# One product of each pair of gate and up units split into seven of half the size, from the fifth unit on

## The chip, the cores and the metric

The kernel runs on one core of a Trainium2 chip. TensorE (PE) multiplies, VectorE (DVE) and ScalarE (ACT) do the element-wise work on PSUM and SBUF, GpSimd (POOL) takes some sums in SBUF, and SyncE (SP) issues most transfers. The metric is the device time of one execution in microseconds.

## The reference

A trunk of two layers over x (1024 tokens, 1024 channels). Each layer has a token mixer (attention) and a SwiGLU channel mixer; the change is in the first half of the channel mixer alone:

```python
x = x + jnp.concatenate([y_tok, y_mem], axis=-1) @ w_out[i]
h = rmsnorm(x, norm_ffn[i])
gu = h @ w_gate_up[i]
x = x + (jax.nn.silu(gu[..., :D_FF]) * gu[..., D_FF:]) @ w_down[i]
```

D_FF is 2816, so gate and up are each 22 units of 128 columns. All is float32; a product is made of three fp32r products of high and low halves (hi and lo: `hi` on ACT rounds, `lo` on DVE takes the rest).

## The kernel before

A layer runs in stages, one after the other, and PE is kept busy across them: the input projection and attention, the output projection, gate and up, and down. Tokens lie along the free axis in two halves of 512 (HS).

Gate and up treat each unit as a 2 x 2 block product in Winograd's form: left are the weights of the unit (g1, g2 the gate's two halves in depth, u1, u2 the up's), right the four blocks of h and their sums, in `B[0]` to `B[6]`. Seven products `n` = 0 to 6 of 4 x 3 matmuls (four blocks in depth, three terms hi x hi, hi x lo, lo x hi) of 128 x 512 take the place of eight. The class `Pair` (L826) holds a unit: `prepare` makes the weights of a product (sums of blocks on POOL into a tile wS, L841 and L848, then hi on ACT and lo on DVE, L106 and L109), `product` (L873, matmuls at L886) adds them into one of two banks X and Y, and `read` (L891) takes the bank to SBUF: g1, g2 (through SiLU), c1, c2. Product 6, the seventh, is u2 times B[6]; its result is taken from c1, and c1 is multiplied by g1.

Units go two by two: when both are done, `hand_over` (L1008) forms the sums that the down stage needs as its right sides and writes them to memory (b_d). The order is a list (L924): the first four units in a mixed order, then each unit's n = 0 to 6. `gate_up` (L1032) goes through it: it calls `prepare` for the entry four places ahead (`lead`), then `product` and `read` of the entry. Loads of weights (`load_gu`, L933) are issued in `prepare` of n = 4 and 6, into five tiles (wgu_raw). A scheduler keeps the written order as a priority, and settles, when the program is built, in which order each engine's instructions stand; each engine then works through its own.

The buffers that matter: weights of n = 2, 3 share one tile (wgu2), of n = 6 one (wgu6, tag w4), of n = 0 and 4 three (wgu); wS has two tiles; results and x live in 21 tiles of 512 columns (tag t2k). In PSUM, X takes one of two banks in each of two pools in turn, Y one of three (ps_t); a further bank (ps_o) is free in this stage.

## Time and profile before

| what | value |
|---|---|
| median of 3 runs | 2156.9 us (2153.25 to 2157.82) |
| the profiled execution | 2155.14 us, its span 2153.4 us |
| granted clock over the span | 0.992 |
| gate and up, fifth unit on, layer 0 | from about 494 us to 838 us |
| the same, layer 1 | from about 1580 us to 1924 us |
| one product of 12 matmuls there | 2.73 us |
| a pair of units there | 14 products, 38.2 us |

The page gives, for each engine, its busy time, and groups of like instructions with their count, mean time and the idle time ahead of them. The windows give the same sums for a stretch of the span. The timeline gives instructions in order of time: start, time, engine, line, what is written and read, how many in a row; in brackets the idle time of the engine before, and what ended it. Rows of matmuls overlap, so the distance from one row's start to the next one's is what a group costs.

### The profile page before, as it was taken

How to read it: one execution, taken by the hardware profiler on the slowest of the kernel's cores; microseconds unless marked ns; L12 is line 12 of the kernel's file. 1: busy time of each engine (PE TensorE's matmuls, PEld its weight loads, DVE VectorE, ACT ScalarE, POOL GpSimd, SP SyncE). 2: the span in 40 equal slices, each digit the busy share in tenths (PEclk: the TensorE clock that was granted, in tenths of full speed). 3: DMA queues.
4: the chain of work that ended last, by engine and by line, in shares of the span. 5: the costliest groups of instructions: out<-in, count | busy, mean ns of one | idle time of the engine just before them, and what ended most of it. 6: DMA issues, size and time to landing. Idle time of an engine off the chain costs nothing.

```text
span 2153.4 us, 27952 instructions
## 1 busy us (share of the span) xinstructions
PE 2111.0 (98%) x9946; PEld 1744.3 (81%) x9946; DVE 1458.7 (68%) x2314; ACT 1045.2 (49%) x1988; POOL 509.5 (24%) x545
## 2 busy tenths in 40 slices
PE   7999999999999999999999999999999999999997
PEld 6788888778888888888778888887888888888886
DVE  7677787786556565866766666667866665567675
ACT  6577785443333334344466665653433333344442
POOL 0344330333333330000233233203233333300000
PEclk9999999999999999999999999999999999999998
DMA  6321118333323336865332212275133323277662
GB/s 247 100 93 44 37 60 287 124 91 100 113 94 117 98 118 225 298 215 201 105 91 66 78 58 72 86 246 168 58 119 117 98 93 113 93 247 261 203 208 93
DMA packets 120076, 287.22 MB, mean 133 GB/s; under 512 B 12288, under 2 KB 18688, under 8 KB 119936
## 3 DMA queue, kind: packets, MB, share of 16 engines
q1 hardware_dynamic: 112896, 272.57, 38.5%
q10 hardware_dynamic: 7040, 12.85, 1.6%
q8 instruction: 79, 1.29, 0.2%
q14 instruction: 61, 0.50, 0.1%
HBM read 210.40 MB, written 68.94 MB: 130 GB/s over the span
## 4 chain that ended last, share of the span: by engine, by line
PE 75%; issue 13%; DVE 4%; ACT 3%; DMA 2%; POOL 2%; DVEq 0%; SPq 0%; ACTq 0%; POOLq 0%
PE X L886 20%; PE Y L886 16%; PE mm L139 14%; PE po L139 6%; PE X L1178 5%; PE Y L1178 4%; PE S L559 3%; PE O L622 3%; PE pT L602 3%; DMA xr_d<-x 1%; DMA x<-in_x 1%; ACT p L574 1%; POOL wS L841 1%; DVE wgu L109 1%; DVE pl L109 0%
## 5 line engine op out<-in xcount | busy, mean ns | idle before, releaser
L109 DVE TENSOR_TENSOR wgu<-wS,wgu 128x1024 fp32r<-128x1024 f32 x88 | 111.0, 1261 | 255.9 <-ACT wgu L106 255.9
L886 PE MATMUL Y<-hB,wgu 128*128 128x512 f32 x1056 | 257.0, 393 | 0.8 <-ACT c L906 0.8
L886 PE MATMUL X<-hB,wgu 128*128 128x512 f32 x1056 | 254.2, 390 | 1.0 <-ACT g L903 1.0
L886 PE MATMUL X<-hT,wgu 128*128 128x512 f32 x1056 | 254.2, 391 | 0.0
L1178 PE MATMUL X<-hB,wd 128*128 128x512 f32 x1056 | 242.4, 390 | 0.9 <-DVE x L1146 0.9
L886 PEld LDWEIGHTS Y<-hB,wgu 128*128 128x128 f32 x1056 | 198.5, 188 | 44.7 <-ACT c L906 1.6
L886 PEld LDWEIGHTS X<-hB,wgu 128*128 128x128 f32 x1056 | 198.4, 188 | 43.9 <-ACT g L903 1.9
L886 PEld LDWEIGHTS X<-hT,wgu 128*128 128x128 f32 x1056 | 198.5, 188 | 42.8
L1178 PEld LDWEIGHTS X<-hB,wd 128*128 128x128 f32 x1056 | 198.0, 188 | 43.1 <-issue 2.3
L587 POOL TENSOR_SCALAR p<-p,stat 128x384 f32<-128x384 f32 (+1 forms) x256 | 141.0, 570 | 313.2 <-DVE stat L584 212.8
L139 PE MATMUL mm<-hT,wqk 128*128 128x512 f32 x672 | 199.9, 405 | 0.1
L139 PE MATMUL po<-yT,wo 128*128 128x512 f32 x768 | 184.7, 394 | 0.0
L1178 PE MATMUL Y<-hB,wd 128*128 128x512 f32 x792 | 180.4, 389 | 0.0
L1178 PEld LDWEIGHTS Y<-hB,wd 128*128 128x128 f32 x792 | 148.5, 188 | 31.2 <-DVE x L1146 0.5
L139 PEld LDWEIGHTS po<-yT,wo 128*128 128x128 f32 x768 | 142.5, 188 | 29.5 <-issue 1.0
L106 ACT CAST wgu<-wS 128x1024 fp32r<-128x1024 f32 x88 | 92.4, 1050 | 131.3 <-POOL wS L841 108.1
L233 POOL TENSOR_TENSOR nr<-nv,neg_half 128x4 f32<-128x4 f32 (+1 forms) x11 | 11.7, 1063 | 598.5 <-DVE nv L232 598.4
L841 POOL TENSOR_TENSOR wS<-wgu_raw 128x512 f32<-128x512 f32 x44 | 65.9, 1498 | 362.9 <-DVE wgu L109 362.9
L106 ACT CAST hB<-b_raw 128x512 fp32r<-128x512 f32 x154 | 89.4, 618 | 112.0 <-DMA b_raw<-b_d 96.0
L574 ACT ACTIVATE p<-p,stat 128x256 f32<-128x256 f32 (+1 forms) x192 | 112.3, 586 | 52.2 <-DVE stat L570 49.5
L109 DVE TENSOR_TENSOR pl<-pT,ph 128x384 fp32r<-128x384 f32 (+1 forms) x256 | 118.7, 494 | 21.8 <-ACT ph L106 18.8
L109 DVE TENSOR_TENSOR hB<-b_raw,hB 128x512 fp32r<-128x512 f32 x154 | 99.8, 686 | 49.5 <-ACT hB L106 49.3
(161 smaller groups left out, 3924.6 us busy)
## 6 DMA issues: line engine op xcount, KB each, us to landing
wgu_raw<-in_w_gu SPq DMA_DIRECT2D x92, 512.0 KB
wd_raw<-in_w_dn SPq DMA_DIRECT2D x70, 512.0 KB
b_raw<-b_d SPq DMA_DIRECT2D x70, 512.0 KB
b_d<-c SPq DMA_DIRECT2D x88, 256.0 KB
b_d<-t SPq DMA_DIRECT2D x66, 256.0 KB
wo_raw<-in_w_out SPq DMA_DIRECT2D x32, 512.0 KB
x<-in_x SPq DMA_DIRECT2D x32, 256.0 KB
xr_d<-x ACTq DMA_DIRECT2D x32, 256.0 KB
```

The source lines that it names most:

```text
L106: nc.scalar.copy(dst, src)
L109: (eng or nc.vector).tensor_tensor(dst, src, h.bitcast(F32), op=ALU.subtract)
L139: nc.tensor.matmul(ps[:, :n], l, r, start=start and i == 0 and j == 0, stop=stop and i == len(order) - 1 and j == 2,)
L233: nc.gpsimd.tensor_tensor(r[:, :nb], v[:, :nb], neg_half[:, :nb], op=ALU.pow)
L559: nc.tensor.matmul(s_[:, :n], Q[self.h][:, qb * P : (qb + 1) * P], k, start=j == 0, stop=j == 1)
L574: nc.scalar.activation(p[:, :n], p[:, :n], AF.Exp, bias=m1, scale=-1.0, accum_out=s1)
L587: nc.gpsimd.tensor_scalar(p[:, :n], p[:, :n], ri[:, i : i + 1], 1.0, op0=ALU.mult, op1=ALU.mult)
L602: nc.tensor.transpose(tr[:, j * P : (j + 1) * P], p[:, j * P : (j + 1) * P], ident)
L622: nc.tensor.matmul(o[:, c0 : c0 + w * P], self.value(j), t[:, s0 : s0 + w].rearrange("p j q -> p (j q)"), start=j == js[0] and t is self.p ...
L841: sub = lambda o, p_, q_: nc.gpsimd.tensor_tensor(o, p_, q_, op=ALU.subtract)
L886: nc.tensor.matmul(ps, l, r, start=n in (0, 1, 3, 6) and k == 0 and i == 0, stop=k == 3 and i == 2, skip_group_check=True,)
L1178: nc.tensor.matmul(bank, l, r, start=i in (0, 1, 3, 6) and p == 0 and n == 0, stop=p == HF - 1 and n == 2, skip_group_check=True,)
```

## The change

From the fifth unit on, the two products n = 6 of a pair of units (a, b) are seen as one 2 x 2 block product of half the size in each direction, and made in Winograd's form again: seven products of 2 x 3 matmuls of 256 columns (class `Fourth`), 42 matmuls for 24 of 512. Left are u2 of both units and four sums of their halves (s1 to s4, on POOL, L942 and L943, in a tile of wS's two); right are quarters of B[6] and the sums t1 to t4. t1 takes the place of a part of B[6]; t2 to t4 are made by `quarters` once per layer, a step after each entry of the order from the last of the first four units on. The weights lie in tiles of t2k, whose number goes from 21 to 24; wgu6's tile is gone.

The seven are done in three groups behind products 4, 5 and 6 of the second unit's count (n = 3, 4, 5): A (two products), B (two), C (three). They use one bank of ps_t (X4) and ps_o (Y4), in which later groups add to what earlier ones left, and after each group DVE takes what is new from the c1 of a and b (L995). Multiplying by g1 and the hand-over follow C. Weight loads that hung on n = 6 are issued, both, in the pair's `Fourth.prepare`, which stands four places ahead of A.

```diff
     tc.tile_pool(name=f"fs{layer}", bufs=1, reuse_waits="tile") as fs,
...
 ):
-    phase[:] = fp, 21, 5
+    phase[:] = fp, 24, 5
     wide[:] = True, 2
     def pair(src, dst):
...
     norms = [Norm(), Norm()]
     B = [[None] * 4 for _ in range(7)]
+    fourth = []
     def load_x(m, f):
...
         nc.sync.dma_start(x[m][f], (a["x"] if is_a else x_d)[m][:, f * HS : (f + 1) * HS])
...
                 w = fp.tile([P, 2, D], F32R, tag="t8", name="wgu8", bufs=6)
...
                 w = fp.tile([P, 2, D], F32R, tag="w8", name="wgu2", bufs=1)
-            elif n == 6 and self.j >= first:
-                w = fp.tile([P, 2, HS], F32R, tag="w4", name="wgu6", bufs=1)
             else:
...
             if n == 6:
...
             elif n == 3:
...
                 nc.scalar.copy(self.c2, Y)
+                if 4 in self.seen:
+                    add(self.c2, self.c2, self.c1)
             elif n == 4:
...
                 nc.scalar.copy(self.c1, X)
-                add(self.c2, self.c2, self.c1)
+                if 3 in self.seen:
+                    add(self.c2, self.c2, self.c1)
                 if 5 in self.seen:
...
             elif n == 5:
...
                 add(self.c1, self.c1, X, ALU.subtract)
                 add(self.c1, self.c1, self.g1, ALU.mult)
+    h2 = HS // 2
+    class Fourth:
+        def __init__(self, a_, b_):
+            self.units, self.w = (a_, b_), None
+        def tile(self):
+            return fp.tile([P, HS], F32R, tag="t2k", name="wgu4", bufs=24)
+        def prepare(self, n):
+            if self.w is not None:
+                return
+            r0, r1 = (u.raw[1][:, HS:] for u in self.units)
+            s = fs.tile([P, D], F32, tag="S", name="wS4", bufs=2)
+            s1, s2, s3, s4 = (s[:, i * h2 : (i + 1) * h2] for i in range(4))
+            sub = lambda o, p_, q_: nc.gpsimd.tensor_tensor(o, p_, q_, op=ALU.subtract)
+            nc.gpsimd.tensor_tensor(s1, r1[:, :h2], r1[:, h2:], op=ALU.add)
+            sub(s2, s1, r0[:, :h2])
+            sub(s3, r0[:, :h2], r1[:, :h2])
+            sub(s4, r0[:, h2:], s2)
+            self.w = []
+            for t in (r0, r1[:, h2:], s[:, :HS], s[:, HS:]):
+                n_ = t.shape[-1]
+                if n_ == HS:
+                    th, tl = self.tile(), self.tile()
+                else:
+                    th = self.tile()
+                    th, tl = th[:, :h2], th[:, h2:]
+                hi(th, t)
+                lo(tl, t, th)
+                for c in range(0, n_, h2):
+                    self.w.append((th[:, c : c + h2], tl[:, c : c + h2]))
+            load_gu()
+            load_gu()
+        def part(self, bank, at, left, right, start=False, stop=False):
+            for k in range(2):
+                kw = [t[:, k * P : (k + 1) * P] for t in left]
+                for i, (l, r) in enumerate(three(kw, right[k])):
+                    nc.tensor.matmul(
+                        bank[:, at : at + h2], l, r, start=start and k == 0 and i == 0,
+                        stop=stop and k == 1 and i == 2, skip_group_check=True,
+                    )
+        def product(self, n):
+            a11, a12, a22, s1, s2, s3, s4 = self.w
+            block = lambda k0, c: [
+                [B[6][k0 + k][:, i, c : c + h2] for i in range(2)] for k in range(2)
+            ]
+            b11, t1, b21, b22 = block(0, 0), block(0, h2), block(2, 0), block(2, h2)
+            t2, t3, t4 = ([[z[:, k] for z in t] for k in range(2)] for t in fourth)
+            if n == "A":
+                self.X = ps_t.tile([P, HS], F32, tag="T", name="X4")
+                self.Y = ps_o.tile([P, HS], F32, tag="O", name="Y4")
+                self.part(self.X, 0, a11, b11, start=True)
+                self.part(self.Y, 0, a12, b21, start=True)
+            elif n == "B":
+                self.part(self.X, 0, s2, t2)
+                self.part(self.Y, h2, s1, t1)
+            else:
+                self.part(self.X, 0, s3, t3)
+                self.part(self.Y, h2, s4, b22, stop=True)
+                self.part(self.X, h2, a22, t4, stop=True)
+        def read(self, n):
+            (a, b), X, Y = self.units, self.X, self.Y
+            low, high = slice(0, h2), slice(h2, HS)
+            sub = lambda c, ps, op=ALU.subtract: nc.vector.tensor_tensor(c, c, ps, op=op)
+            if n == "A":
+                sub(a.c1[:, low], X[:, low])
+                sub(a.c1[:, low], Y[:, low])
+            elif n == "B":
+                sub(a.c1[:, high], X[:, low])
+                sub(b.c1[:, high], Y[:, high])
+            else:
+                sub(
+                    b.c1.rearrange("p (n c) -> p n c", n=2),
+                    X[:, low].unsqueeze(1).to_broadcast([P, 2, h2]),
+                )
+                sub(a.c1[:, high], Y[:, high])
+                sub(b.c1[:, low], X[:, high], ALU.add)
+                for u in self.units:
+                    sub(u.c1, u.g1, ALU.mult)
     us = [Pair(j) for j in range(NF)]
...
     order = [(u, n) for u in us[:first] for n in (0, 1)]
-    for j in range(0, first, 2):
-        order += [(u, n) for n in (3, 2, 5, 4, 6) for u in us[j : j + 2]]
-    order += [(u, n) for u in us[first:] for n in range(7)]
+    for j in range(0, NF, 2):
+        a_, b_ = us[j : j + 2]
+        z = Fourth(a_, b_)
+        if j < first:
+            order += [(u, n) for n in (3, 2, 5, 4, 6) for u in (a_, b_)]
+        else:
+            order += [(a_, n) for n in range(6)] + [(b_, n) for n in range(4)]
+            order += [(z, "A"), (b_, 4), (z, "B"), (b_, 5), (z, "C")]
     loads = [(us[j], 0) for j in range(first)] + [(us[0], 1), (us[1], 1)]
     loads += [(u, i) for u in us[2:] for i in range(2)]
...
             B[6][k] = pair(x[k + 4][0], t_op(k))
             yield
+    def quarters():
+        sub = lambda o, p_, q_: nc.vector.tensor_tensor(o, p_, q_, op=ALU.subtract)
+        t2, t3, t4 = (temp("q4").rearrange("p (k c) -> p k c", k=2) for _ in range(3))
+        for k in range(2):
+            top, bottom = x[k + 4][0], x[k + 6][0]
+            sub(t3[:, k], bottom[:, h2:], top[:, h2:])
+            sub(top[:, h2:], top[:, h2:], top[:, :h2])
+            sub(t2[:, k], bottom[:, h2:], top[:, h2:])
+            sub(t4[:, k], t2[:, k], bottom[:, :h2])
+            yield
+        for t in (t2, t3, t4):
+            f = [fp.tile([P, 2, h2], F32R, tag="t2k", name="q4h", bufs=24) for _ in range(2)]
+            hi(f[0], t)
+            lo(f[1], t, f[0])
+            fourth.append(f)
+            yield
+        for k in range(2):
+            t = B[6][k]
+            hi(t[:, 0, h2:], x[k + 4][0][:, h2:])
+            lo(t[:, 1, h2:], x[k + 4][0][:, h2:], t[:, 0, h2:])
+            yield
     def keep(i, p, t):
         nc.sync.dma_start(b_d[layer][i][:, p * HS : (p + 1) * HS], t)
...
         keep(6, p, o)
     lead = 4
-    rest = right_sides()
+    rest, more = right_sides(), quarters()
     def gate_up():
         run_some(rest, 1)
...
             u.product(n)
...
             run_some(rest, 1 if i < 2 * first else 2)
-            if n == 6 and u.j % 2:
+            if i >= 7 * first - 1:
+                run_some(more, 1)
+            if n == "C":
+                hand_over(u.units[0].j // 2, *u.units)
+            elif n == 6 and u.j % 2:
                 hand_over(u.j // 2, us[u.j - 1], u)
-            yield u, n
+            yield i - len(order)
     wd = a["w_dn"][layer].rearrange("(p i) r c -> p i r c", i=2)
...
         if last:
             nc.scalar.dma_start(out[:2].rearrange("k p t -> p k t")[:, :, at:], first)
-    for u, n in gate_up():
-        if u.j == NF - 1 and n in (2, 3, 4):
-            keep_rows(n - 2)
-            if n > 2:
-                left_side(0, n - 3)
-        if u.j == NF - 1 and n in (3, 4, 5):
-            right_side(0, n - 3)
+    for to_go in gate_up():
+        if -7 <= to_go <= -5:
+            keep_rows(to_go + 7)
+            if to_go > -7:
+                left_side(0, to_go + 6)
+        if -6 <= to_go <= -4:
+            right_side(0, to_go + 6)
     norms = [Norm(), Norm() if is_a else Norm(HS, 7)]
...
     parts = iter(())
```

How the instructions stand now, at three places. Numbers in names tell buffers apart; the rows are of one pair in layer 0. L894 of before is L893 now, L1012 is L1130.

DVE, in the second unit of a pair, before: from the addition of n = 1 (g1) to the product by g1. wgu2_5610, wgu_5658 and wgu_5712 are weights of the next unit.

```order
L894 TENSOR_TENSOR g1_5538<-Y_5540,g1_5538 128x512 [waits DMAHW3_49,PE_49,Activation_49]
L109 TENSOR_TENSOR wgu2_5610<-wS_5607,wgu2_5610 128x1024 [waits PE_49,Activation_49]
L1012 TENSOR_TENSOR t1_5645<-c1_5480,c2_5466 128x512 [waits DMAHW6_49,DVE_49]
L894 TENSOR_TENSOR c2_5590<-c2_5590,c1_5604 128x512 [waits Activation_49]
L109 TENSOR_TENSOR wgu_5658<-wS_5607,wgu_5658 128x1024 [waits Activation_49]
L894 TENSOR_TENSOR g2_5572<-Y_5577,g2_5572 128x512 [waits DMAHW4_49,PE_49]
L109 TENSOR_TENSOR wgu_5712<-wgu_raw_5434,wgu_5712 128x1024 [waits DMAHW6_49,Activation_49]
L894 TENSOR_TENSOR c2_5590<-c2_5590,g2_5572 128x512 [waits Activation_49]
L894 TENSOR_TENSOR c1_5604<-c1_5604,X_5525 128x512 [waits DMAHW5_49,PE_49]
L109 TENSOR_TENSOR wgu6_5693<-wgu_raw_5399,wgu6_5693 128x512 [waits DMAHW4_49,Activation_49]
L894 TENSOR_TENSOR c1_5604<-c1_5604,g1_5538 128x512 [waits DVE_49]
```

And now, at the same place (c1_5547 is the first unit's, c1_5686 the second's; wgu2_5706, wgu_5763 and wgu_5798 are weights of the next pair):

```order
L893 TENSOR_TENSOR g1_5602<-Y_5611,g1_5602 128x512 [waits DMAHW2_49,PE_49,Activation_49]
L995 TENSOR_TENSOR c1_5547<-c1_5547,X4_5655 128x256 [waits PE_49]
L995 TENSOR_TENSOR c1_5547<-c1_5547,Y4_5656 128x256 [waits DVE_49,PE_49]
L109 TENSOR_TENSOR wgu2_5706<-wS_5703,wgu2_5706 128x1024 [waits Activation_49]
L995 TENSOR_TENSOR c1_5547<-c1_5547,X4_5655 128x256 [waits PE_49]
L109 TENSOR_TENSOR wgu_5763<-wS_5703,wgu_5763 128x1024 [waits Activation_49]
L893 TENSOR_TENSOR c2_5653<-c2_5653,c1_5686 128x512 [waits DMAHW5_49,Activation_49]
L995 TENSOR_TENSOR c1_5686<-c1_5686,Y4_5656 128x256 [waits DMAHW6_49,DVE_49,PE_49]
L893 TENSOR_TENSOR g2_5638<-Y_5640,g2_5638 128x512 [waits DMAHW4_49,PE_49]
L109 TENSOR_TENSOR wgu_5798<-wgu_raw_5585,wgu_5798 128x1024 [waits DMAHW2_49,Activation_49]
L893 TENSOR_TENSOR c2_5653<-c2_5653,g2_5638 128x512 [waits Activation_49]
```

The two lo of wS_5703 stand between the reads of X4 and Y4 after groups A and B, and the last read of B, of Y4 into c1_5686, stands behind both and behind the sum of c2.

ACT, before: from the copy of n = 4 of a first unit to the SiLU of n = 1 of the second.

```order
L909 COPY c1_5480<-X_5401 128x512 [waits PE_49]
L106 CAST wgu_5520<-wS_5483 128x1024 [waits Pool_49]
L106 CAST wgu_5574<-wgu_raw_5296 128x1024 [waits DMAHW2_49,PE_49,Activation_49]
L915 ACTIVATE g2_5448<-g2_5448 128x512 [waits DVE_49]
L106 CAST wgu6_5555<-wgu_raw_5261 128x512 [waits DMAHW0_49,PE_49,Activation_49]
L897 COPY g1_5538<-X_5525 128x512 [waits DMAHW3_49,PE_49]
L900 ACTIVATE g1_5538<-g1_5538 128x512 [waits DVE_49]
```

And now, the same stretch:

```order
L910 COPY c1_5547<-X_5467 128x512 [waits PE_49]
L106 CAST wgu4_5570<-wgu_raw_5144 128x512 [waits DMAHW3_49,DMAHW0_49]
L106 CAST wgu_5606<-wS_5529 128x1024 [waits Pool_49]
L106 CAST wgu4_5574<-wgu_raw_5286 128x256 [waits DMAHW5_49,DMAHW0_49]
L106 CAST wgu4_5577<-wS4_5565 128x512
L106 CAST wgu_5671<-wgu_raw_5308 128x1024 [waits DMAHW1_49,PE_49,Activation_49]
L917 ACTIVATE g2_5512<-g2_5512 128x512 [waits DVE_49]
L106 CAST wgu4_5581<-wS4_5565 128x512
L896 COPY g1_5602<-X_5589 128x512 [waits DMAHW2_49,PE_49]
L899 ACTIVATE g1_5602<-g1_5602 128x512 [waits DVE_49]
```

Casts for the seven products (wgu4) stand around the cast of wgu_5606, the second unit's weights of n = 4 and 5, all ahead of the copy of X_5589 (n = 0).

PE, before: the end of n = 4, then n = 5 and n = 6 of a second unit.

```order
L886 MATMUL X_5525<-hB_4802,wgu_5520 128x512 x3
L886 MATMUL Y_5577<-hB_4705,wgu_5520 128x512 [waits Activation_49]
L886 MATMUL Y_5577<-hB_4705,wgu_5520 128x512 x2
L886 MATMUL Y_5577<-hB_4730,wgu_5520 128x512 x3
L886 MATMUL Y_5577<-hB_4733,wgu_5520 128x512 x3
L886 MATMUL Y_5577<-hB_4758,wgu_5520 128x512 x3
L886 MATMUL X_5525<-hT8_4805,wgu6_5555 128x512 [waits Activation_49]
L886 MATMUL X_5525<-hT8_4805,wgu6_5555 128x512
L886 MATMUL X_5525<-hT8_4805,wgu6_5555 128x512 [waits DVE_49]
L886 MATMUL X_5525<-hT8_4805,wgu6_5555 128x512 x3
L886 MATMUL X_5525<-hT8_4829,wgu6_5555 128x512 x6
```

And now: the end of n = 5, then group C up to its second bank.

```order
L967 MATMUL Y4_5656<-hT8_4805,wgu4_5578 128x256
L885 MATMUL Y_5640<-hB_4705,wgu_5606 128x512 [waits Activation_49]
L885 MATMUL Y_5640<-hB_4705,wgu_5606 128x512 x2
L885 MATMUL Y_5640<-hB_4730,wgu_5606 128x512 x3
L885 MATMUL Y_5640<-hB_4733,wgu_5606 128x512 x3
L885 MATMUL Y_5640<-hB_4758,wgu_5606 128x512 x3
L967 MATMUL X4_5655<-q4h_5201,wgu4_5581 128x256 [waits DVE_49]
L967 MATMUL X4_5655<-q4h_5202,wgu4_5581 128x256
L967 MATMUL X4_5655<-q4h_5201,wgu4_5582 128x256
L967 MATMUL X4_5655<-q4h_5201,wgu4_5581 128x256
L967 MATMUL X4_5655<-q4h_5202,wgu4_5581 128x256
L967 MATMUL X4_5655<-q4h_5201,wgu4_5582 128x256
L967 MATMUL Y4_5656<-hT8_4829,wgu4_5581 128x256 [waits DVE_49]
```

Each bank's first matmul of C waits for DVE, where n = 6 waited for ACT's copy of n = 4 and for its weights.

## The prediction

> **What bounds the kernel now.** I read the page first, then the stages by windows, then one pair of units in the timeline.
>
> ```profile
> span 2153.4 us, 27952 instructions
> PE 2111.0 (98%) x9946; PEld 1744.3 (81%) x9946; DVE 1458.7 (68%) x2314; ACT 1045.2 (49%) x1988; POOL 509.5 (24%) x545
> ...
> 489.00:814.00 325.00, 325.00 (x1432) 268.76 (x1431) 197.02 (x208) 119.49 (x170) 102.43 (x65) 1.00 0.33 108
> 1575.00:1907.00 332.00, 332.00 (x1463) 274.54 (x1462) 201.01 (x212) 121.73 (x173) 104.37 (x66) 1.00 0.33 108
> ```
>
> The two windows (length, then busy time of PE, PEld, DVE, ACT, POOL; clock 1.00) are gate and up from the fifth unit on, in both layers, where the change lies. PE has no idle time there: 325.00 of 325.00 us. So a column less is time won, and a wait of PE is time lost; nothing else counts. DVE has 39% idle on average, but it serves its queue in order, and so does ACT. What that means is seen where the stage ends:
>
> ```profile
> 828.79 0.60 ACT L106 CAST hB<-b_raw 128x512 fp32r<-128x512 f32 x1
> 829.30 0.58 ACT L903 COPY g<-X 128x512 f32<-128x512 f32 x1
> 829.93 3.04 PE L886 MATMUL X<-hB,wgu 128*128 128x512 f32 x12 [0.65 <-ACT g L903]
> 832.81 2.89 PE L886 MATMUL Y<-hB,wgu 128*128 128x512 f32 x12
> ```
>
> The copy that frees bank X stood in ACT's queue behind a cast whose transfer was late, and PE stood 0.65 us; the group took 3.04 us for 2.89, so a restart costs some 0.1 us besides.
>
> **The change, part by part.** *TensorE.* Per pair it removes 24 matmuls of 512 columns (product 7 of two units) and adds 42 of 256. What one costs is the distance of starts, not its row's length:
>
> ```profile
> 499.31 2.89 PE L886 MATMUL X<-hT,wgu 128*128 128x512 f32 x12
> 502.04 2.89 PE L886 MATMUL Y<-hT,wgu 128*128 128x512 f32 x12
> ...
> 36.80 4.37 PE L139 MATMUL mm<-mhl,wm 128*128 128x256 f32 x35
> ...
> L139 PE MATMUL mm<-mhl,wm x192: 274/285/679, 5.9 to 44.4; 128*128 128x256 f32 x192
> ```
>
> 512 columns: 2.73/12 = 0.227 us. 256 columns, an undisturbed run of the memory projection, fp32r with a new weight load for each, as here: (4.37 - 0.285)/34 = 0.120 us, more than half of 0.227. So 24 x 0.227 = 5.45 us become 42 x 0.120 = 5.04: 0.40 us a pair, 18 pairs (nine a layer): **7.3 us**, where an eighth of the columns would have been 12.3. The Trainium skill (TensorE: Matmul & The Clock Gate, section "Wait — 56ns, not 53.3ns?") gives a warm spacing of columns by 2.4 GHz and 2.5 ns more, an estimate of 109 ns at 256 columns and 216 at 512; the trace has 227 at 512, so it doesn't agree, and by that rule product 7 would save about 0.87 us a pair before any wait.
>
> *What stands beside PE.* DVE's new work per pair, by these rows: six reads of 256 columns and one of 512 in place of two of 512; three rests of 512 and one of 256 in place of two of 512.
>
> ```profile
> L337 DVE TENSOR_TENSOR mt<-mm,mscale 128x256 f32<-128x256 f32 x8 | 3.2, 415 | 0.0
> ...
> 539.00 0.68 DVE L1012 TENSOR_TENSOR c<-c,c 128x512 f32<-128x512 f32 x1
> 539.60 0.68 DVE L1012 TENSOR_TENSOR t<-t,c 128x512 f32<-128x512 f32 x1
> ...
> L109 POOL TENSOR_TENSOR wqk<-wqk_raw,wqk 128x256 fp32r<-128x256 f32 x12 | 8.4, 739 | 7.5 <-ACT wqk L106 7.5
> ...
> 514.34 0.60 ACT L106 CAST wgu<-wgu_raw 128x512 fp32r<-128x512 f32 x1
> ```
>
> 6 x 0.415 - 0.68 + 0.68 + 0.415 = 2.9 us on DVE, which goes from 197.02/325 x 38.2 = 23.2 to 26 of a pair's 38.2; ACT +1.0; POOL four sums, 4 x 0.74 = 3.0. All of it fits under PE by amount. The sums of T2 to T4, once a layer, are 8 x 0.415 + 3 x 0.68 + 2 x 0.415 = 6.2 us of DVE; behind the first four units DVE sits idle for 5.02 us up to 506.53 (row below), and A of the first pair comes eight products behind the 499.31 row, at 521, so I put them at nothing; uncovered they would be 12 us over both layers. No byte of DMA is added, but the two weight loads that hung on product 7 go behind the second unit's sums and the first rest of product 7, and on SP ahead of the hand-over's writes:
>
> ```profile
> 510.85 0.33 SPq L937 DMA_DIRECT2D wgu_raw<-in_w_gu  x1
> ...
> 514.51 1.53 POOL L848 TENSOR_TENSOR wS<-wgu_raw 128x512 f32<-128x512 f32 x1 [3.69 <-DMA wgu_raw<-in_w_gu]
> ```
>
> From issue to the sum that waits for it, 3.7 us. They go out some 28 us into the pair by the reckoning below, land at 32, and what they feed is cast 22 us into the next pair, at 60: nothing, and the rival of a late load falls with it.
>
> *The new wait.* Group C writes into the second half of Y4 after DVE has read group B there. In DVE's order that read stands fourth behind others, of which two belong to the next pair: the rests (lo halves) of its weights for n = 2, 3 (wgu2) and n = 4, 5. The second waits for ACT's cast, this for POOL's two sums, these for the first rest, since both use one tile wS; and the first waits for the end of n = 3 of the second unit, as wgu2 is one buffer. Before, this chain ran at leisure:
>
> ```profile
> 506.53 1.22 DVE L109 TENSOR_TENSOR wgu<-wS,wgu 128x1024 fp32r<-128x1024 f32 x1 [5.02 <-ACT wgu L106]
> ...
> 523.84 2.89 PE L886 MATMUL X<-hB,wgu 128*128 128x512 f32 x12
> 524.04 0.59 ACT L906 COPY c<-Y 128x512 f32<-128x512 f32 x1 [2.14 <-PE Y L886]
> 524.52 1.05 ACT L106 CAST wgu<-wS 128x1024 fp32r<-128x1024 f32 x1
> 525.61 1.23 DVE L109 TENSOR_TENSOR wgu<-wS,wgu 128x1024 fp32r<-128x1024 f32 x1 [6.11 <-ACT wgu L106]
> 526.91 1.66 POOL L841 TENSOR_TENSOR wS<-wgu_raw 128x512 f32<-128x512 f32 x1 [9.17 <-DVE wgu L109]
> 527.39 1.74 DVE L894 TENSOR_TENSOR c<-c,c 128x512 f32<-128x512 f32 x1
> 528.54 1.74 POOL L841 TENSOR_TENSOR wS<-wgu_raw,wS 128x512 f32<-128x512 f32 x1
> 530.32 1.05 ACT L106 CAST wgu<-wS 128x1024 fp32r<-128x1024 f32 x1 [2.96 <-POOL wS L841]
> 531.39 1.23 DVE L109 TENSOR_TENSOR wgu<-wS,wgu 128x1024 fp32r<-128x1024 f32 x1 [2.27 <-ACT wgu L106]
> ...
> 482.93 1.30 POOL L848 TENSOR_TENSOR wS<-wgu_raw 128x512 f32<-128x512 f32 x1 [1.46 <-DMA wgu_raw<-in_w_gu]
> 484.31 1.29 POOL L841 TENSOR_TENSOR wS<-wS,wgu_raw 128x512 f32<-128x512 f32 x1
> ```
>
> Product n = 3 ended at 523.84; the second rest ended 8.78 us later, with nobody waiting. The two sums took 3.37 us there, in turns with a DVE addition of two SBUF operands (1.74 us for 0.68); alone a sum takes 1.29.
>
> Now with that end as zero. PE: A, 12 x 0.120, to 1.44; n = 4 to 4.17; B to 5.61; n = 5 to 8.34; the first six of C to 9.06. There it needs the read. DVE: X4 of A at 0.92, Y4 of A from 1.64 (0.20 us after PE, as 524.04 after 523.84) to 2.06; the first rest, ready at 1.77, starts at 1.98 (queue neighbours overlap by 0.08, the 539.00 and 539.60 rows) and ends at 3.21; POOL from 3.27, undisturbed, since the one DVE instruction in that time reads PSUM: 2 x 1.29 = to 5.81; cast at 5.85; rest 1.07 later, 6.92 to 8.15; c2 + c1 to 8.75; the read of Y4, which waits for the end of that, 8.79 to 9.20; PE at 9.25. PE stands 9.25 - 9.06 = 0.19, and with the restart **0.30 us a pair**. Bounds: with the sums at 3.37 instead of 2.54 it is 1.13; were the chain 0.2 shorter, nothing.
>
> A second place is ACT's queue in the second unit: its copy of n = 0 (needed by n = 2, which adds to the same bank) stands behind the cast of its own weights for n = 4, 5, three casts for product 7 and a SiLU. By the same durations from the end of the first unit's n = 3: cast at 6.1, rest to 8.4, DVE's g2 addition to 9.0, SiLU to 9.7, cast 0.60, copy to 10.7; PE needs it at 4 x 2.73 = 10.9. It just fits; I put it at nothing, 0.5 us a pair if it doesn't.
>
> The last pair of a layer has no next pair behind it, but the casts of the next stage; there PE lost about 0.7 us before and by the same reckoning does so now.
>
> Sum: -18 x 0.404 + 16 x 0.30 = -7.3 + 4.8 = **-2.5 us** against the profiled execution's own 2155.14 us (span 2153.4), that is 2152.6; the median of the runs shown, 2156.9, lies 1.8 above it, so I give **2154.4**.
>
> **The rivals.** *No wait at C.* If the chain is only 0.2 us shorter than I make it, all 7.3 us come in: 2156.9 - 7.3 = 2149.6. For it: 0.19 us is 2% of a chain of ten links. Against: each link has its row, and the pair repeats identically.
>
> *The chain is longer: slower.* The sums of the next pair's weights on POOL meet DVE again, or the first rest starts late because DVE is still in its backlog before A (three rests of product 7 in turns with POOL's sums). At the price of the 526.91 to 530.28 rows, 0.83 us, PE waits 1.13 a pair: 16 x 1.13 - 7.3 = +10.8, 2167.7. It decides from 0.1 us over my chain (then the saving is gone); beyond 0.37 it is slower by over 0.2%. For it: in the rows shown these sums never ran alone, and DVE carries 2.9 us more. Against: in the new order nothing with two SBUF operands stands between the two rests.
>
> *ACT's queue.* The 0.5 us of the second place on top of mine: +9 - 2.5 = +6.5, 2163.4; I count it with the slower one.
>
> **How the numbers follow.** Mine 0.42, no wait 0.31, longer chain or ACT's queue 0.27. About 0.2%, 4.3 us, is what a measurement of this kernel can tell from no change. Of mine (-2.5, give or take 4) 0.05 is faster, 0.04 slower, the rest the same; no wait is faster; of the slower ones 0.03 stay within. So faster 0.36, same 0.36, slower 0.28. The range goes from 2148 (no wait, and a little at the stage's end) to 2167, near the dearer chain; mine alone 2150 to 2159.
>
> **What would show it.** In the timeline of the new stage: 256-column groups at 0.120 us between starts (0.114 would add 4.5 us of saving); PE idle before a Y4 matmul of C, released by DVE's c1, of about 0.2 us in every pair but the last; the first rest ending about 3.2, the second about 8.2 us after n = 3. PE busy in 489 to 814 falls below the window only by these. It is wrong if PE shows no such gap (then 2149.6), or gaps over 0.5 us, or one released by ACT's copy of g1.

## Result: a little slower, 1.0015 of before

The changed kernel takes 2156.4 us (median; 2151.3 to 2163.2), the kernel before, timed beside it, 2153.1: ratio 1.0015, interval 1.0008 to 1.0022, so 3.3 us slower (1.7 to 4.7) where 2.5 us faster was forecast. The 2156.9 us on which the forecast stands is the median of three executions; of the 22 beside the changed kernel it is 2153.1. The profiled execution of the changed kernel is the longest of its times, 2163.15 us (span 2161.3); a second profile of it, among the experiments, is of an execution of 2158.2 us (span 2156.4).

The page of the changed kernel, its span and the first lines by engine:

```profile
span 2161.3 us, 28955 instructions
PE 2114.2 (98%) x10270; PEld 1758.0 (81%) x10270; DVE 1514.0 (70%) x2466; ACT 1060.8 (49%) x2034; POOL 578.5 (27%) x617
```

And the window of gate and up from the fifth unit on, the same stretch of time as the prediction's first row of windows:

```profile
489.00:814.00 325.00, 324.34 (x1577) 273.17 (x1576) 220.90 (x279) 127.88 (x192) 135.76 (x101) 1.00 0.30 106
```

DVE goes from 197.02 to 220.90 us here, 2.8 a pair (forecast 2.9); POOL from 102.43 to 135.76, 3.9 a pair (forecast 3.0). PE's busy time, 324.34 of 325.00 us, does not show what a pair costs. Its length does: from the first matmul of one pair to that of the next. The last pair is counted to 0.227 us behind the start of its last matmul; where that has 256 columns, as in the changed kernel, this is 0.11 us more than up to the first matmul of the down stage, here and below.

| us | before | changed | changed, second profile |
|---|---|---|---|
| pairs 1 to 8 of a layer, each | 38.16 | 38.13 | 38.13 |
| last pair, first layer | 39.12 | 41.45 | 41.73 |
| last pair, second layer | 38.82 | 44.56 | 42.17 |

So the sixteen steady pairs did almost what was forecast (38.16 - 0.404 + 0.30 = 38.06 was expected), and the two last pairs, put down with the saving of 0.404 and otherwise as before, lost 2.3 to 5.7 us each.

### The steady pair: the forecast wait, where it was expected

The timeline of the changed kernel, one second unit; n = 3 ends at the start of the first row (the columns are start, length, engine, line, operation, and in brackets the idle time and who ended it):

```profile
597.62 0.88 PE L967 MATMUL X<-hT,wgu 128*128 128x256 f32 x6
...
599.25 0.42 DVE L995 TENSOR_TENSOR c<-c,Y 128x256 f32<-128x256 f32 x1 [0.30 <-PE Y L967]
599.59 1.22 DVE L109 TENSOR_TENSOR wgu<-wS,wgu 128x1024 fp32r<-128x1024 f32 x1
600.89 1.29 POOL L842 TENSOR_TENSOR wS<-wgu_raw 128x512 f32<-128x512 f32 x1 [2.98 <-DVE wgu L109]
...
602.14 1.30 POOL L842 TENSOR_TENSOR wS<-wgu_raw,wS 128x512 f32<-128x512 f32 x1
...
603.47 1.05 ACT L106 CAST wgu<-wS 128x1024 fp32r<-128x1024 f32 x1 [4.12 <-POOL wS L842]
...
604.55 1.23 DVE L109 TENSOR_TENSOR wgu<-wS,wgu 128x1024 fp32r<-128x1024 f32 x1 [1.41 <-ACT wgu L106]
605.69 0.69 DVE L893 TENSOR_TENSOR c<-c,c 128x512 f32<-128x512 f32 x1
...
606.47 0.42 DVE L995 TENSOR_TENSOR c<-c,Y 128x256 f32<-128x256 f32 x1
...
606.95 0.78 PEld L967 LDWEIGHTS Y<-hT,wgu 128*128 128x128 f32 x6 [0.28 <-DVE c L995]
606.95 0.98 PE L967 MATMUL Y<-hT,wgu 128*128 128x256 f32 x6
```

Every link of the worked chain is there. The first rest ends 3.19 us after n = 3 (3.21 forecast), the second 8.16 (8.15), the read 9.27 (9.20), PE goes on at 9.33 (9.25), and the sums on POOL ran alone at 1.29 and 1.30. The start of the six matmuls into Y4 is 0.24 us late, and the group takes 0.98 instead of 0.88: with the distances of starts, 0.35 us a pair, for 0.30 forecast.

### The last pair: two pauses, then half the clock

The same view of the last pair of the second layer:

```profile
1917.41 1.29 DVE L109 TENSOR_TENSOR hB<-b_raw,hB 128x512 fp32r<-128x512 f32 x2 [3.33 <-ACT hB L106]
1918.17 1.05 ACT L106 CAST wd<-wd_kept 128x1024 fp32r<-128x1024 f32 x1 [0.27 <-DMA wd_kept<-in_w_dn]
...
1919.26 1.23 DVE L109 TENSOR_TENSOR wd<-wd_kept,wd 128x1024 fp32r<-128x1024 f32 x1 [0.55 <-ACT wd L106]
1920.40 0.41 DVE L995 TENSOR_TENSOR c<-c,X 128x256 f32<-128x256 f32 x1
...
1920.87 0.98 PE L967 MATMUL X<-q4h,wgu 128*128 128x256 f32 x6 [1.53 <-DVE c L995]
1921.20 1.05 ACT L106 CAST wd<-wd_kept 128x1024 fp32r<-128x1024 f32 x1 [1.50 <-DMA wd_kept<-in_w_dn]
...
1922.28 1.23 DVE L109 TENSOR_TENSOR wd<-wd_kept,wd 128x1024 fp32r<-128x1024 f32 x1 [1.47 <-ACT wd L106]
1923.42 0.41 DVE L995 TENSOR_TENSOR c<-c,Y 128x256 f32<-128x256 f32 x1
...
1923.89 1.65 PE L967 MATMUL Y<-hT,wgu 128*128 128x256 f32 x6 [2.05 <-DVE c L995]
...
1925.34 4.88 PE L885 MATMUL Y<-hB,wgu 128*128 128x512 f32 x12
```

Group A of this pair ended at 1916.4, but DVE reads X4 only at 1920.40: the read stands behind two rests of the right side, for which DVE had waited 3.33 us, and behind the rest of the first down weights, this behind ACT's cast, and this behind a transfer (the bracket of the 1918.17 row). The read of Y4 stands behind a second rest, which waited for the next transfer. PE stood 1.69 and 2.21 us (1.14 and 0.65 in the first layer, by the same spacing). And behind the pauses product n = 5 took 4.88 us for 2.9. The windows around both places, with the granted clock as the third number from the end:

```profile
830.50:833.80 3.30, 1.83 (x13) 1.39 (x12) 3.30 (x6) 2.33 (x5) 0.00 (x0) 1.00 1.03 398
833.90:837.20 3.30, 3.30 (x11) 2.62 (x10) 1.70 (x4) 0.20 (x1) 0.00 (x0) 0.50 0.95 328
1919.40:1922.70 3.30, 0.98 (x6) 0.78 (x6) 1.83 (x3) 1.80 (x3) 0.00 (x0) 1.00 1.03 398
1922.80:1929.50 6.70, 5.61 (x16) 4.74 (x17) 3.51 (x7) 1.14 (x2) 0.00 (x0) 0.50 0.65 237
```

The clock is 0.50 for one stretch of 3.41 us in the first layer and for two in the second; matmuls of 512 columns then start 0.427 us apart instead of 0.227. The kernel before has no such stretch in the last pairs.

### The profile page after: what moved, and what is told of

Its sections match the earlier page's. It is cut to its first block, busy times and chain, and to the rows that moved or that the text cites. A ratio compares the mean times of both kernels' runs of the same rounds, so it can differ in the third digit from the quotient of the medians.

```text
span 2161.3 us, 28955 instructions
## 1 busy us (share of the span) xinstructions
PE 2114.2 (98%) x10270; PEld 1758.0 (81%) x10270; DVE 1514.0 (70%) x2466; ACT 1060.8 (49%) x2034; POOL 578.5 (27%) x617
## 5 line engine op out<-in xcount | busy, mean ns | idle before, releaser
L885 PE MATMUL Y<-hB,wgu 128*128 128x512 f32 x1056 | 261.6, 398 | 0.8 <-ACT c L905 0.8
L109 DVE TENSOR_TENSOR wgu<-wS,wgu 128x1024 fp32r<-128x1024 f32 (+1 forms) x124 | 153.4, 1237 | 130.5 <-ACT wgu L106 130.4
L106 ACT CAST wgu<-wS 128x1024 fp32r<-128x1024 f32 (+1 forms) x124 | 114.3, 923 | 148.0 <-POOL wS L842 124.6
L885 PE MATMUL X<-hT,wgu 128*128 128x512 f32 x624 | 150.2, 391 | 0.0
L842 POOL TENSOR_TENSOR wS<-wgu_raw 128x512 f32<-128x512 f32 x44 | 61.0, 1387 | 299.6 <-DVE wgu L109 299.6
L885 PEld LDWEIGHTS X<-hT,wgu 128*128 128x128 f32 x624 | 116.8, 188 | 26.3
```

The costliest lines, as they stand in the source:

```text
L106: nc.scalar.copy(dst, src)
L109: (eng or nc.vector).tensor_tensor(dst, src, h.bitcast(F32), op=ALU.subtract)
L842: sub = lambda o, p_, q_: nc.gpsimd.tensor_tensor(o, p_, q_, op=ALU.subtract)
L885: nc.tensor.matmul(ps, l, r, start=n in (0, 1, 3, 6) and k == 0 and i == 0, stop=k == 3 and i == 2, skip_group_check=True,)
```

## The experiments

Theory: two losses with two separate causes. One is the wait at C in each steady pair, from the place of the read of Y4 in DVE's queue behind the second rest. The other is in the last pair, where DVE's reads of X4 and Y4 stand behind the next stage's rests. The rival: the added work on DVE and POOL costs time everywhere, and no single place bears it.

### The last pair in the old order

```
+    elif j == NF - 2:
+        order += [(u, n) for u in (a_, b_) for n in range(7)]
...
-    if -7 <= to_go <= -5:
-        keep_rows(to_go + 7)
+    if -5 <= to_go <= -3:
+        keep_rows(to_go + 5)
```

> Undoes the change in the last pair of each layer alone (units 20 and 21): there all seven products stand in the old order again, and the next stage's loads and casts stand where they stood before; the other eight pairs of a layer keep the new order. Theory (the loss lies in the last pair, where DVE's reads of X4 and Y4 behind group A stand in its queue behind rests of the down weights, and the pauses of TensorE that follow bring the granted clock down to 0.5): the last pairs, 41.45 and 44.56 us in the profiled execution of the change, come back to about 39 (39.12 and 38.82 before), no stretch of clock 0.5 at the end of a stage, the eight steady pairs stay at 38.13, and the whole is about 2152.5 us, 0.5 below the kernel before: ratio 1.000. Rival (the cost is spread, by more load on DVE and POOL in every pair, and the long last pair is only where a late chain comes out): the last pair of the old order is late too, or other pairs grow; ratio stays near 1.0015.

Measured: 2150.0 us, ratio to before 0.9985 (0.9976 to 0.9994). The last pairs take 38.30 us in both layers, the steady ones 38.14, and no stretch at the end of the stage has clock 0.5. So 6.4 us of the changed kernel's time stand in the last pairs. (This kernel leaves out one step, the turning back of T1 into B12 ahead of the last pair; the run with B12 restored has it.) The last pairs came out shorter than the old kernel's (39.12, 38.82), because PE does not stand there now as it did at 829.93 in the kernel before; why not was not followed further.

### The matmuls into Y4 last in group C

```
 self.part(self.X, 0, s3, t3)
-self.part(self.Y, h2, s4, b22, stop=True)
 self.part(self.X, h2, a22, t4, stop=True)
+self.part(self.Y, h2, s4, b22, stop=True)
```

> One line moved: within group C the six matmuls into Y4 (s4 with B22) go behind the six into X4 (A22 with t4), so TensorE needs DVE's read of Y4 0.72 us later. Theory (TensorE stands 0.24 us and 0.105 for the restart in each steady pair, for the read of Y4 alone, with nothing else late there): the wait goes, the steady pairs take 38.13 - 0.35 = 37.78 us, 16 of them 5.5 us less than the change; the last pairs stay as long as in the change; about 2151 us, ratio near 0.999. Rival (the wait only moves, to the read of X4, to DVE's next read of Y or to the weights behind it): pairs stay at 38.1, ratio near 1.0015.

Measured: 2149.7 us, 0.9985 (0.9976 to 0.9994). Each steady pair takes 37.79 to 37.82 us; the timeline of this kernel:

```profile
602.31 0.42 DVE L995 TENSOR_TENSOR c<-c,Y 128x256 f32<-128x256 f32 x1
...
603.26 0.88 PE L967 MATMUL Y<-hT,wgu 128*128 128x256 f32 x6
```

The read is as late as before, and ends 0.53 us ahead of the matmuls that need it: no bracket, 0.88 us for six. With this wait gone, 38.16 - 37.79 = 0.37 us is what the seven half-size products save in a pair (0.404 forecast). The last pairs stay long, 40.19 and 39.32 us, with pauses of 1.43 and 0.65 us, and of 0.57 and 0.65, this time without a lower clock.

### Both

> Both edits together: the last pair of each layer in the old order, and the six matmuls into Y4 last in group C in the other pairs. Theory (the two losses have separate causes and add): steady pairs 37.78, last pairs about 39, about 2147 us, 6 below the kernel before, ratio 0.997. Rival (one cause behind both, or the time comes back at another place): not below the better of the two alone.

Measured: 2145.3 us, 0.9962 (0.9950 to 0.9975): steady pairs 37.79 to 37.82, last pairs 38.30. The two gains, 6.4 and 6.7 us against the changed kernel, add to 13.1; together they gave 11.1. For the missing 2 us the last pairs of the run with the Y4 matmuls moved are a likely place, 79.5 us in its profile against 83.9 in the changed kernel's second: with shorter pauses and without the lower clock they had won part of the other edit's gain already. The sizes, 4.4 us and 2, do not match, so this is not shown.

### More work on POOL, and another place in DVE's queue

```
 if n == 4:
+    if self.j >= first:
+        sub(s[:, HS : HS + 256], g1[:, :256], u1[:, :256])
     sub(s[:, HS:], g1, u1)
```

> Adds work, and takes nothing away: one more subtraction of 128x256 on POOL ahead of the sums for product n = 4 of each unit from the fifth on; what it writes is written over by the sum behind it, so it is of no use. 36 times about 0.74 us on POOL. It makes the scheduler place DVE's reads behind group B, and c2 + c1, ahead of the second rest of the next pair's weights, where the change has them behind it. Theory (the wait at C comes from the place of the read in DVE's queue, behind that rest, and not from how much DVE and POOL have to do): the wait at C goes although POOL does more, steady pairs 37.78 us, last pairs as in the change or somewhat longer, about 2151 us, ratio near 0.999. Rival (the length of the chain or the load of POOL sets it): the wait grows by the added 0.74 us to about 1.08 in each steady pair, 38.87 us, about 12 us more than the change: 2168, ratio 1.007.

Measured: 2148.2 us, 0.9975 (0.9965 to 0.9985). One unit in its timeline:

```profile
596.98 0.74 POOL L842 TENSOR_TENSOR wS<-wgu_raw 128x256 f32<-128x256 f32 x1 [2.81 <-DVE wgu L109]
...
599.77 0.41 DVE L997 TENSOR_TENSOR c<-c,Y 128x256 f32<-128x256 f32 x1
...
601.78 1.23 DVE L109 TENSOR_TENSOR wgu<-wS,wgu 128x1024 fp32r<-128x1024 f32 x1 [1.60 <-ACT wgu L106]
```

The added instruction is the first row. The second rest ends 9.3 us after n = 3, later than in the changed kernel, and nobody waits for it: the read of Y4 is done 1.6 us before it starts, since it now stands before it in the queue. Steady pairs take 37.83 to 37.89 us (the first of each layer 38.59). More work, and the wait at C is gone: the place in the queue decided, not the amount.

Its last pairs are a test that was not planned. Both take the read of X4 behind A ahead of the first down rest; the first layer's takes 38.0 us, the second's 39.66, with a pause of 1.49 us before group C, where DVE stood behind two rests of the right side that waited for a transfer.

### Both, with B12 restored

The last pair in the old order multiplies B12, in whose place the change keeps T1, so the two runs with that order worked with T1 in one quarter of product 7's right side there. This one puts it right:

```
+    for k in range(2):
+        add(z[:, k], t[:, 0, :h2], t[:, 0, h2:])
+        add(z[:, k], z[:, k], t[:, 1, :h2])
+        add(z[:, k], z[:, k], t[:, 1, h2:])
+        hi(B[6][k][:, 0, h2:], z[:, k])
+        lo(B[6][k][:, 1, h2:], z[:, k], B[6][k][:, 0, h2:])
```

> As the run with both edits (last pair of each layer in the old order; in group C the matmuls into Y4 last), with one step more behind the ninth unit pair's predecessor: T1, which the new order keeps in the place of B12 in the fourth block of the right side, is turned back into B12 (T1 + B11: per layer six additions, two casts and two rests of 256 columns on DVE and ACT), since the old product 7 multiplies B12. In the runs of the last pair in the old order without it (the last pair alone, and both edits), this one quarter of product 7's right side held T1 in the last pair: same instructions, other numbers. Theory (10 small instructions of 0.4 us beside 38 us of matmuls are hidden): as the run with both edits, 2145.3 us, ratio 0.996. Rival (DVE is late again at the start of the last pair): some 2 to 3 us more, 2148.

Measured: 2145.8 us, 0.9965 (0.9953 to 0.9978); last pairs 38.30. The added sums are hidden.

### Group B one product later in the last pair

```
+    if j < NF - 2:
         order += [(z, "A"), (b_, 4), (z, "B"), (b_, 5), (z, "C")]
+    else:
+        order += [(z, "A"), (b_, 4), (b_, 5), (z, "B"), (z, "C")]
```

> On top of the moved Y4 matmuls of group C: in the last pair of each layer alone, product 5 of the second unit goes ahead of group B (A, 4, 5, B, C for A, 4, B, 5, C), so that two products, 5.5 us, stand between A and B for DVE's reads of X4 and Y4. All work of the next stage stays as it is. Theory (the last pair is long because those reads, queued behind the rests of the down weights, come 2.1 us (first layer) and 1.2 us (second) later than B can take them): the waits before B go, the last pairs come from 40.2 and 39.3 to about 38, less a wait between B and C that this order brings (C writes into the half of X4 that B's read frees: up to 0.5 us); about 2147.5, 2 under the run with only the Y4 matmuls moved. Rival (the whole queue of DVE and ACT is late by what the next stage adds, so the wait only moves to C): last pairs stay at 39 to 40, about 2149.7.

Measured: 2148.4 us, 0.9978 (0.9969 to 0.9987), which the intervals do not tell from the run without it. The last pairs take 40.60 and 40.35 us, of which 0.7 us each are three matmuls of the down stage that stand among C's: the rival's result. PE no longer stands before B, but 0.82 and 0.43 us before product 5, and 1.01 and 1.13 between B and C. The second wait is again for DVE's reads. The first is not:

```profile
822.64 1.05 ACT L106 CAST wd<-wd_kept 128x1024 fp32r<-128x1024 f32 x1 [0.24 <-DMA wd_kept<-in_w_dn]
...
823.60 0.58 ACT L905 COPY c<-Y 128x512 f32<-128x512 f32 x1
...
824.23 3.03 PE L885 MATMUL Y<-hB,wgu 128*128 128x512 f32 x12 [0.66 <-ACT c L905]
```

Product 5 waits for ACT's copy of n = 3, which stands in ACT's queue behind the casts of the next stage. So ACT's queue is late here too; in the order A, 4, B, 5, C nobody waits for that copy. More distance for one group's reads only moved the wait: what makes DVE and ACT late is still in their queues.

### The changed kernel again

> The changed kernel again, for a second profile of it. Theory (TensorE's two pauses before the parts of group B of the last pair are in every execution, since they come from the order of DVE's queue; the clock of 0.5 behind them is only in some, and makes the highest of its times): last pairs of 40 to 41.5 us, with pauses of 0.6 to 1.7 us before X4 and 0.65 to 2.2 us before Y4 and, if the clock stays at 1.0 there, 2154 to 2157 us. Rival (the clock is lowered in every execution): 0.5 again in the last pairs.

One execution, 2158.2 us. The theory's half on the clock fell:

```profile
828.00:831.30 3.30, 1.57 (x10) 0.95 (x9) 3.21 (x5) 2.44 (x5) 0.00 (x0) 1.00 1.04 402
831.40:834.70 3.30, 3.30 (x12) 2.82 (x12) 2.18 (x5) 0.58 (x2) 0.00 (x0) 0.50 0.69 237
1916.90:1920.20 3.30, 1.24 (x9) 0.82 (x7) 2.80 (x4) 2.85 (x4) 0.00 (x0) 1.00 1.04 403
1920.30:1923.60 3.30, 2.91 (x11) 2.44 (x10) 3.05 (x7) 1.14 (x2) 0.00 (x0) 0.50 0.70 274
```

Pauses of 1.40 and 0.65 us, and of 2.22 and 0.65, and behind them clock 0.50 in both layers again. What the lower clock costs is 0.2 us for each 512-column matmul in it, and by the distances of starts, the 256-column ones included, 1.6 and 1.2 us here, 1.6 and 2.6 in the first profile; the rest of the last pairs' loss are the pauses themselves, with a restart of 0.1 us behind each.

### The next stage's rests off DVE, in two steps

First the rests of the first two down weight pairs go to POOL, everything else as with the Y4 matmuls moved:

```
+    if i == 0 and g < 2:
+        nc.gpsimd.tensor_tensor(two(w[:, 1], n), src, two(w[:, 0], n), op=ALU.subtract)
+    else:
         lo(two(w[:, 1], n), src, two(w[:, 0], n))
```

> On top of the moved Y4 matmuls of group C: the rests (lo halves) of the first two weight pairs of the down stage go from DVE to POOL, with everything else as in the changed kernel (order A, 4, B, 5, C in the last pair too). DVE's reads of X4 and Y4 behind group A then stand right behind the rests of the right side (hB). Theory (in the last pair these reads are late because they stand in DVE's queue behind two rests of 1.23 us that wait for ACT's casts, and these for a transfer): both pauses of TensorE, 1.43 + 0.65 us and 0.57 + 0.65 us in the run with only the Y4 matmuls moved, go; what may stay is a wait at C behind the right side's transfers (1.49 us once, in the run with the longer POOL work); last pairs 38 to 39.3, about 2147 us, 2 to 3 under that run's 2149.7. Rival (ACT's queue or the transfers themselves make TensorE wait, or the wait moves to C in full, as with group B moved): last pairs stay at 39.3 to 40.5, about 2149.7.

Measured: 2150.9 us, 0.9984 (0.9973 to 0.9995). The last pairs stay at 40.53 and 39.59 us, but PE stands elsewhere. First layer:

```profile
825.90 0.42 DVE L995 TENSOR_TENSOR c<-c,Y 128x256 f32<-128x256 f32 x1
...
826.12 0.88 PE L967 MATMUL X<-q4h,wgu 128*128 128x256 f32 x6
...
829.47 2.95 DVE L109 TENSOR_TENSOR hB<-b_raw,hB 128x512 fp32r<-128x512 f32 x2 [0.46 <-ACT hB L106]
...
832.34 0.41 DVE L995 TENSOR_TENSOR c<-c,X 128x256 f32<-128x256 f32 x1
...
832.80 1.70 PE L967 MATMUL X<-q4h,wgu 128*128 128x256 f32 x12 [2.34 <-DVE c L995]
```

Before group B nothing waits any more. But the reads behind B, needed by C, stand behind the next rests in the queue, those of the right side (hB), which take 2.95 us for 1.29 while POOL works. PE stands 2.5 us there (1.6 in the second layer); 1.7 us of this (0.9) are the longer rests, which the edit itself brought. The theory is right in its first half, the rival in the time. If the queue is the cause, these two rests must go as well:

```
+    lo(t[:, 1], raw[:, q], t[:, 0], nc.gpsimd if i == 0 and g == 2 else None)
```

> On top of the run with the rests of two weight pairs on POOL: the two rests of the right side (hB) that stand in DVE's queue between the reads behind group A and those behind group B go to POOL as well. Now nothing of the next stage stands in DVE's queue between group A's reads and group B's. Theory (the last pair is long only because DVE's reads of X4 and Y4 queue behind the next stage's rests, whichever these are): the pause at C, 2.50 and 1.61 us, goes too; last pairs about 37.9 to 38.2, that is 4 us less in both layers, unless POOL's late rests (four rests of 1.3 to 2.6 us) hold up the start of the down stage; 2146 to 2148 us. Rival (ACT or the transfers bind there, and a wait stays at C or behind it): last pairs stay at 39.5 to 40.5, about 2151.

Measured: 2144.8 us, 0.9962 (0.9948 to 0.9975). Last pairs 38.21 and 37.91. DVE in the first layer's, with PE's group C:

```profile
822.98 0.42 DVE L995 TENSOR_TENSOR c<-c,X 128x256 f32<-128x256 f32 x1
...
823.50 0.42 DVE L995 TENSOR_TENSOR c<-c,Y 128x256 f32<-128x256 f32 x1
...
826.52 0.41 DVE L995 TENSOR_TENSOR c<-c,X 128x256 f32<-128x256 f32 x1
826.85 0.41 DVE L995 TENSOR_TENSOR c<-c,Y 128x256 f32<-128x256 f32 x1
...
827.73 1.60 PE L967 MATMUL X<-q4h,wgu 128*128 128x256 f32 x12
...
828.82 3.53 POOL L109 TENSOR_TENSOR hB<-b_raw,hB 128x512 fp32r<-128x512 f32 x2
```

The first read, of X4 behind A, still stands behind two rests of the right side that waited for a cast, and group B starts 0.2 us late; the others come in time, and POOL's late rests hold up nobody. What was late moves off the path, and the time follows: against the kernel before, timed beside each, 3.5 us less became 8.1, a gain of some 4.5 us (the two intervals just touch), of which the last pairs show 4.0. This version and the one with the old order in the last pair, the Y4 matmuls last and B12 restored beat both kernels; they cannot be told apart.

How far the pairs alone explain the medians (pairs of a profile summed over both layers against the 688.5 us of before; medians against the kernel before, timed beside each):

| | pairs, us | medians, us |
|---|---|---|
| changed (second profile) | +5.4 | +3.3 |
| old order in the last pair | -1.7 | -3.2 |
| Y4 matmuls last in C | -4.2 | -3.5 |
| POOL's added work | -3.8 | -5.0 |
| old order and Y4 last, B12 restored | -7.2 | -7.7 |
| group B one product later (without the three matmuls of the down stage in each last pair) | -4.3 | -5.0 |
| two down rests on POOL | -3.7 | -3.5 |
| all four rests on POOL | -7.7 | -8.1 |

They agree to 2.1 us. What is left over lies outside this stage and was not settled.

## Why the prediction was wrong

**What bounds the kernel.** Right: PE is the path, and a column less is time won. With the waits out of the way the saving came in: 8.1 us (2144.8), where 7.3 was worked out; of the 7.7 us that the pairs show, 1.8 stand in the last pairs, where the old order's own wait went too.

**The saving.** 0.37 us a pair by the pairs' length, 0.404 worked out; that a half-size matmul costs more than half (0.120 for 0.227) held, the groups in the changed kernel run at it. The 0.87 us that the prediction estimates by the Trainium skill (TensorE: Matmul & The Clock Gate, section "Wait — 56ns, not 53.3ns?") takes 0.227 us at 512 columns from the trace and 109 ns at 256 from the rule; by the rule for both the estimate is 0.6, and the runs show 0.37.

**The new wait at C.** The right place, the right chain, each link within 0.1 us. The restart, put at 0.11, was 0.105 (the row that it was read from, 3.04 for 2.89, has 0.15 at 512 columns). The term was 0.35 us instead of 0.30. By the pairs' lengths sixteen of them gain 0.5 us in all where 1.7 was forecast. The rival without a wait was wrong, and so was the longer chain: POOL's sums took 1.29 and 1.30 us. The distances at which that rival decides, 0.1 and 0.37 us, do not follow from its own 16 pairs: over these the saving is gone 0.16 us over the chain, and 0.2% is passed at 0.43.

**ACT's queue, the quarters, the loads.** Each put at nothing, and no pause shows at any of the three places; the first pair of a layer, where the quarters are made, is as long as the others.

**The last pair.** This is the step that failed: "there PE lost about 0.7 us before and by the same reckoning does so now". Measured are 2.3 to 2.6 us more in the first layer and 3.4 to 5.7 in the second, 6.0 to 8.1 together, where the forecast gain of the whole was 2.5. The reckoning carried over a wait of the old order (ACT's copy behind a cast, 0.65 us) to a pair in which PE now waits for six reads of DVE, and did not walk DVE's queue at this place as it did in the steady pair. There two down rests and two rests of the right side stand ahead of and between the reads, and these wait for casts and transfers, which the added distance of one product did not cover (40.60 and 40.35 us). Taking these four out of that queue brought the last pairs from 40.19 and 39.32 to 38.21 and 37.91 us. The pauses also lowered the clock, 2.8 us of the last pairs in the second profile and 4.2 in the first, for which no term stood in the sum.

**The range.** 2156.4 lies in it, but by luck, for a reason none of the rivals named; the slower rival's mechanism, a longer chain at C, was not the one.

## What to carry to other kernels

When a change lets the matrix engine wait for short reads on an in-order engine, walk that engine's queue at every place where the order differs, and above all at the seam to the next stage: here one pair in nine lost 2.3 to 5.7 us, and the eight others together gained 0.2. A read that frees a bank belongs ahead of work for later stages that waits for transfers; where the order cannot be had directly, give that work to another engine, or issue the matmuls that need the read last. And two short pauses close together can cost more than their length.

## Of the hardware, unexpected

Pauses of 1 to 2 us lowered the granted clock. The four drops of the changed kernel's last pairs stand behind stretches of 3.41 us in which PE was busy for 0.98 to 1.83 us (the window rows above). But length alone does not decide. In the run with two down rests on POOL, PE stood 2.50 us in one piece (from 830.30 to the 832.80 row), longer than any of those, and the clock stayed at 1.00. Its windows, cut where the stretches of 3.41 us begin when they are counted back from that run's changes of clock:

```profile
828.50:831.80 3.30, 1.96 (x9) 1.30 (x7) 2.84 (x3) 2.19 (x3) 2.77 (x1) 1.00 1.04 400
831.90:835.20 3.30, 2.40 (x19) 2.40 (x20) 3.30 (x6) 1.49 (x3) 0.00 (x0) 1.00 0.98 374
```

The pause lies across two stretches, and in neither was PE busy for less than 1.96 us. In the same way the pauses of 1.43 and 0.65 us with the Y4 matmuls moved, equal to those of the changed kernel's second profile, fell into two stretches (2.03 us busy in the first) and lowered nothing, where the latter fell into one. So what a pause costs besides its length seems to hang on where it fell; these few executions are all that shows it.

The Trainium skill (TensorE: Matmul & The Clock Gate, section "Part 1: The HAM clock gate (the "warmup" mystery)") describes a free-running window of 3413 ns, with half rate after an idle one. The free-running window and the half rate agree with these traces (the drops of the changed kernel's two last pairs begin 1088.85 us apart, which is 319 times 3.413; the clock is 0.50 in both); that the window must be idle does not, since PE was busy for up to 1.83 of 3.3 us ahead of a drop. Nor is a limit between 1.83 and 1.96 us shown: at the start of gate and up the kernel before, too, went to 0.50, behind a window with PE busy for 2.40 us:

```profile
413.70:417.00 3.30, 2.40 (x15) 1.85 (x14) 2.06 (x3) 0.59 (x1) 3.04 (x2) 1.00 0.34 134
417.10:420.40 3.30, 3.30 (x9) 2.11 (x7) 0.69 (x1) 0.00 (x0) 1.02 (x1) 0.50 0.00 0
```

What the rule counts there is open.
